# Odd mixer of an encoder kernel: both halves of a pair's scores as one bound run

## The chip, the cores and the metric

The kernel runs on one core of a Trainium2 chip. The metric is the device time of one execution in microseconds, as the median of several runs. A profiled execution gives a trace besides: its span goes from the first to the last instruction of the program.

The engines are named as the profile names them: PE is TensorE (matrix products; PEld is its loading of weights), DVE is VectorE, ACT is ScalarE, POOL is GpSimd, SP is the queue that issues most loads.

## What is computed

The program is a four-part encoder layer, twice: feed-forward, token mixer, attention into a memory, feed-forward, each followed by a layer norm. There are 512 tokens of width 1024, in 8 rows of 64 columns. The change lies in the token mixer of the second layer (the odd one), a neighbourhood attention with 16 heads of 64: each token looks at all 8 rows and at 16 columns around its own, with a learned bias.

```python
q, k, v = jnp.split(h @ w_in, 3, axis=-1)
...
s = jnp.einsum('bwhd,bawjhd->bhwaj', q_r, k_nb).astype(jnp.float32) * scale
s = s + bias.astype(jnp.float32)[None]
p = jax.nn.softmax(s.reshape(B, C_HEADS, GRID_W, kh * kw), axis=-1)
...
return jnp.einsum('bhwaj,bawjhd->bwhd', p, v_nb)
```

## The kernel before

**Precision.** Operands are split into a high and a low part (`split`: ScalarE makes the high part, VectorE the rest), and a product is the sum of three, high by high, high by low, low by high.

**The odd mixer (`mixer_c`).** Heads go in pairs, eight of them. The two heads of a pair lie on partitions 0 to 63 and 64 to 127 of their tiles of queries and keys, so a product of one head uses half of TensorE's rows (the profile writes 64*128), and products of the two heads can stand side by side. Per pair the loop records: the keys of the next pair (`keys`, into a "t" bank), the transposes of this pair's softmax weights (`turned`, four "t" banks), the queries of the pair after next (`queries`, a "d" bank), the scores of the next pair (`weights_of`), this pair's attention products (`attend`, a "d" bank; 64 output columns per head, which the profile writes 128*64), and two blocks of values for a later pair (`values`, "t" banks; pairs 0 to 5). From pair 6 on parts of the output projection (`down_steps`) stand in place of the work that runs out.

**Scores.** The 512 queries are four blocks of 128 tokens (16 columns of 8 rows). Block t meets `C_BLOCKS[t]`: 24 or 32 columns of keys, so products of 192 or 256 columns. Two blocks make a half, with one PSUM bank per head. Each block takes three products per head, and the two heads alternate: 12 products a half. VectorE adds the bias and finds the smallest value (`tensor_tensor_reduce`; in the order of instructions below these rows are called ISA), and ScalarE takes the exponential.

**PSUM.** The eight banks are shared out by tag: `BUFS` gives "a" three, "d" two, "t" three.

**What sets the order.** The code above only records operations (line 160 issues them all, so that the profile shows one line, and groups go by tile). `plan` is a list scheduler: each engine has a queue of operations that can start, with costs from `cost`; a buffer of a tag is granted in the order in which tiles were recorded, when all users of its last tile are done; an operation can start when its operands and the buffers of the tiles it uses are there. `emit` plans once, works out due times and plans again, then issues.

**Bound runs.** `join(n)` binds the last n operations: each depends on the one before, the first (the leader) takes over all operands' waits of the others, and the others get rank -1, that is, they go first as soon as they can start. Buffers are not part of this: an operation waits for a buffer only if it is itself a user of a tile in it. Before the change each half of the scores is bound by itself (12), and the leader uses one of the half's two banks. The attention products are bound too (8), with one bank.

Of the kernel before, what the change touches and what calls it, by code (L numbers as in the profile page):

```python
# [65 lines left out]
class Graph:  # L66
# [118 lines left out]
    def join(self, n):  # L185

        run = self.ops[-n:]
        for prev, op in zip(run, run[1:]):
            run[0].deps |= op.deps.difference(run)
            op.deps.add(prev)  # L190
            op.rank = -1
        run[0].ns += self.TURN
        run[-1].ns += self.TURN

# [139 lines left out]
class Kernel:  # L334
# [953 lines left out]
    def mixer_c(self, ln_i, last):  # L1288
        nc, a = self.nc, self.a
# [37 lines left out]
        def biases(pair):  # L1327

            table, inner = self.t2(F32), self.t2(F32)
            got = []  # L1330
            for s in range(2):
                tab = table[:, s * 256 : s * 256 + 256]
                nc.gpsimd.dma_start(out=tab, in_=self.bias[2 * pair + s])
                outer = self.t2(F32)
                dst = [outer[:, 0:192], inner[:, s * 256 : s * 256 + 256], outer[:, 192:384]]
                for i, off in enumerate((64, 0, 0)):
                    n = dst[i].shape[1]
                    nc.gpsimd.tensor_tensor(
                        out=dst[i].rearrange("p (u r) -> p u r", r=8),
                        in0=self.near[:, i, : n // 8].rearrange("p (u o) -> p u o", o=1).broadcast_to([P, n // 8, 8]),  # L1340
                        in1=tab[:, off : off + n].rearrange("p (u r) -> p u r", r=8),
                        op=ALU.subtract,
                    )
                got.append(dst)
            return got

        def weights_of(pair):

            tables, q, k = biases(pair), qs.pop(pair), ks.pop(pair)
            both = [[self.t2(F32), self.t2(F32)] for _ in range(2)]  # L1350
            sums = [self.small(4, "l4") for _ in range(2)]
            us = [[], []]
            for z in both:
                nc.gpsimd.memset(z[0][:, 0:64], 0.0)
                nc.gpsimd.memset(z[1][:, 448:512], 0.0)
            for half in range(2):
                ps = [self.ps("a") for _ in range(2)]
                for t in (2 * half, 2 * half + 1):
                    kc, w, _ = C_BLOCKS[t]
                    lo, n = (t % 2) * 256, w * ROWS  # L1360
                    for i, (x, y) in enumerate(((0, 0), (0, 1), (1, 0))):
                        for s in range(2):
                            own = slice(64 * s, 64 * s + 64)
                            nc.tensor.matmul(
                                ps[s][:, lo : lo + n], q[x][own, t * P : (t + 1) * P], k[y][own, kc * 8 : kc * 8 + n],
                                start=i == 0 and t % 2 == 0, stop=i == 2, skip_group_check=True,
                            )
                nc.join(12)
                for t in (2 * half, 2 * half + 1):
                    _, w, kind = C_BLOCKS[t]  # L1370
                    lo, n = (t % 2) * 256, w * ROWS
                    c0 = lo + (64 if t == 0 else 0)
                    for s in range(2):
                        u = both[s][half][:, c0 : c0 + n]
                        mn = self.small(1, "mn")
                        nc.vector.tensor_tensor_reduce(
                            out=u, in0=ps[s][:, lo : lo + n], in1=tables[s][kind], scale=1.0, scalar=3e38, op0=ALU.add,
                            op1=ALU.min, accum_out=mn,
                        )
                        nc.scalar.activation(u, u, AF.Exp, bias=mn, scale=-1.0, accum_out=sums[s][:, t : t + 1])  # L1380
                        us[s].append(u)
            for l, u4 in zip(sums, us):
                nc.vector.reciprocal(l, l)
                for t, u in enumerate(u4):
                    self.normalise(u, l[:, t : t + 1])
            return [[z[:, c * 256 : c * 256 + 256] for z in pair for c in range(2)] for pair in both]
# [50 lines left out]
        keys(0, True)  # L1437
        queries(1)
        us = weights_of(0)
        for pair in range(8):  # L1440


            if pair < 7:
                keys(pair + 1)
            else:
                steps(4)
            pts = turned(us)
            if pair < 6:
                queries(pair + 2)
            else:  # L1450
                steps(5 if pair == 6 else 3)
            if pair < 7:
                us = weights_of(pair + 1)
            if pair == 5:
                out.append(self.staged(self.down_steps(hs, w_out, 0, 256, 1.0 / ALPHA, [], False, alone=True)))
                steps(3)
            attend(pts, pair)
            if pair == 6:
                self.memory_tokens()
            if pair < 6:  # L1460
                for t in range(2):
                    values(pair // 2 + 1, 2 * (pair % 2) + t)
            elif pair == 6:
                steps(4)
# [242 lines left out]
```

## Time and profile before

| what | value |
|---|---|
| median of 3 runs | 2109.37 us (2108.8 to 2109.52) |
| profiled execution | 2108.22 us |
| its span | 2106.4 us |
| TensorE busy | 2086.6 us, 99% |
| VectorE busy | 1754.1 us, 83% |
| ScalarE busy | 1149.9 us, 55% |
| GpSimd busy | 308.4 us, 15% |
| granted TensorE clock | 0.998 |

TensorE is the engine that has almost no idle time. Products are pipelined: a record lasts longer than the distance to the next one, so the rate is read from starts, not from durations. In a timeline a row gives the start in microseconds from the span's start, the length from the first start to the last end of the records that it merges, engine, line, operation, tile written <- tiles read, and the count; a bracket gives the idle time ahead and what ended it.

### The profile page before, as it was taken

Reading aid. Unit: us, or ns where it says so; the run is one execution under the profiler, and the core shown is the slowest. Engines: PE = TensorE matmul, PEld = TensorE weight load, DVE = VectorE, ACT = ScalarE, POOL = GpSimd, SP = SyncE. Lnnn points to the kernel's source line nnn. Section 1 sums busy time; section 2 is a strip of 40 time slices with the busy share of each in tenths; the row PEclk is TensorE's granted clock in tenths of the full one; section 3 lists DMA queues with packets and bytes.
Section 4 is the critical chain, followed back from the end, with each engine's and each line's share of the span. In section 5 each row is a group of like instructions: output and inputs, shape, how many; then the busy total and the mean of one; then the engine's idle time right before and its main releaser. Section 6 shows DMA issues by size and latency. Waiting matters only on the chain.

```text
span 2106.4 us, 33063 instructions
## 1 busy us (share of the span) xinstructions
PE 2086.6 (99%) x13044; PEld 1847.4 (88%) x13044; DVE 1754.1 (83%) x2515; ACT 1149.9 (55%) x1847; POOL 308.4 (15%) x389
## 2 busy tenths in 40 slices
PE   9999999999999999999999999999999999999997
PEld 7999988777888999998999999888878889989996
DVE  7789988788758999998999999754487489999996
ACT  5555543697555655544554545346564466544551
POOL 0001015310002100000310000512131011100002
PEclk9999999999999999999999999999999999999999
DMA  7566562004443566555366656232234433566651
GB/s 208 154 156 153 138 192 84 21 21 140 130 126 95 140 158 183 116 146 165 105 150 161 149 123 189 80 106 76 99 85 148 141 100 115 126 155 156 148 143 60
DMA packets 207868, 270.70 MB, mean 129 GB/s; under 512 B 9184, under 2 KB 156256, under 8 KB 207712
## 3 DMA queue, kind: packets, MB, share of 16 engines
q1 hardware_dynamic: 171200, 211.69, 32.1%
q0 software_dynamic: 36224, 56.63, 15.4%
q8 instruction: 102, 1.67, 0.3%
q14 instruction: 54, 0.44, 0.1%
q10 hardware_dynamic: 288, 0.26, 0.0%
HBM read 266.46 MB, written 4.19 MB: 128 GB/s over the span
## 4 chain that ended last, share of the span: by engine, by line
PE 95%; DVE 3%; DMA 1%; issue 0%; ACT 0%; POOL 0%; DVEq 0%; ACTq 0%; POOLq 0%; SPq 0%
PE a L160 56%; PE d L160 23%; PE t L160 15%; DVE slab L160 1%; DMA slab<-ffn_w_up 1%; DVE x L160 1%; DMA slab<-ffn_w_gate 0%; ACT slab L160 0%; DVE t L160 0%; DVE xl L160 0%; DMA raw<-x_t 0%; POOL rms8y L160 0%; ACT junk L160 0%; POOL slab L160 0%; ACT t L160 0%
## 5 line engine op out<-in xcount | busy, mean ns | idle before, releaser
L160 DVE TENSOR_TENSOR slab<-slab,slab 128x1024 fp32r<-128x1024 f32 (+2 forms) x617 | 732.7, 1212 | 34.7 <-ACT slab L160 26.3
L160 PE MATMUL a<-slab,slab 128*128 128x256 f32 (+3 forms) x2480 | 592.9, 316 | 0.1
L160 ACT CAST slab<-slab 128x1024 fp32r<-128x1024 f32 (+2 forms) x457 | 465.9, 1038 | 180.2 <-DVE slab L160 75.9
L160 PE MATMUL a<-xh,slab 128*128 128x256 f32 (+2 forms) x2384 | 518.1, 307 | 0.3 <-ACT slab L160 0.3
L160 PE MATMUL a<-raw,slab 128*128 128x256 f32 x2432 | 460.9, 283 | 4.6 <-DVE t L160 4.1
L160 PEld LDWEIGHTS a<-slab,slab 128*128 128x128 f32 (+1 forms) x2480 | 422.2, 190 | 41.8 <-issue 3.6
L160 PEld LDWEIGHTS a<-xh,slab 128*128 128x128 f32 x2384 | 395.3, 191 | 26.2 <-ACT slab L160 1.2
L160 PEld LDWEIGHTS a<-raw,slab 128*128 128x128 f32 x2432 | 388.6, 192 | 11.8 <-DVE t L160 6.0
L160 PE MATMUL a<-xl,slab 128*128 128x256 f32 (+2 forms) x1192 | 366.0, 307 | 0.0
L160 PE MATMUL d<-slab,t 128*128 128x512 f32 x1104 | 278.6, 392 | 0.0
L160 PEld LDWEIGHTS a<-xl,slab 128*128 128x128 f32 x1192 | 227.2, 191 | 14.2 <-DVE xl L160 0.2
L160 PEld LDWEIGHTS d<-slab,t 128*128 128x128 f32 x1104 | 199.9, 189 | 36.9 <-issue 0.4
L160 PE MATMUL t<-slab,t 128*128 128x512 f32 x828 | 208.9, 392 | 0.3 <-DVE x L160 0.3
L160 PEld LDWEIGHTS t<-slab,t 128*128 128x128 f32 x828 | 149.5, 189 | 27.7 <-issue 0.7
L160 DVE TENSOR_TENSOR slab<-raw,slab 128x1024 fp32r<-128x1024 f32 (+2 forms) x144 | 158.7, 1126 | 15.7 <-ACT slab L160 15.6
L160 PE MATMUL d<-slab,slab 128*128 128x512 f32 (+3 forms) x736 | 167.4, 416 | 0.0
L160 PEld LDWEIGHTS d<-slab,slab 128*128 128x128 f32 (+1 forms) x736 | 106.2, 170 | 35.4 <-issue 12.9
L160 ACT CAST slab<-raw 128x1024 fp32r<-128x1024 f32 (+1 forms) x128 | 120.2, 968 | 30.9 <-DMA raw<-ab_w_in 9.6
L160 DVE SCALAR_TENSOR_TENSOR x<-d,x 128x512 f32<-128x512 f32 x174 | 118.7, 685 | 19.9 <-PE d L160 18.6
L160 ACT COPY t<-a 128x512 f32<-128x512 f32 (+1 forms) x124 | 68.8, 559 | 115.2 <-PE a L160 73.2
L160 DVE TENSOR_TENSOR t<-a,t 128x512 f32<-128x512 f32 (+1 forms) x100 | 64.3, 645 | 54.8 <-PE a L160 47.3
L160 POOL DMA_DIRECT2D slab<-ffn_w_down x40 | 47.7, 1193 | 294.0 <-DVE slab L160 256.4
(131 smaller groups left out, 2410.1 us busy)
## 6 DMA issues: line engine op xcount, KB each, us to landing
slab<-ffn_w_gate SPq DMA_DIRECT2D x89, 512.0 KB
slab<-ffn_w_up SPq DMA_DIRECT2D x89, 512.0 KB
slab<-ffn_w_down SPq DMA_DIRECT2D x80, 512.0 KB
slab<-ffn_w_down POOLq DMA_DIRECT2D x40, 512.0 KB, 5.8
raw<-mem_w_kv SPq DMA_DIRECT2D x16, 1024.0 KB
slab<-ffn_w_gate POOLq DMA_DIRECT2D x19, 512.0 KB, 6.8
slab<-ffn_w_up POOLq DMA_DIRECT2D x19, 512.0 KB, 6.0
raw<-mem_w_q SPq DMA_DIRECT2D x8, 1024.0 KB
```

The costliest lines, as they stand in the source:

```text
L160: op.call = lambda: fn(*args, **kw)
```

## The change

Two edits. In `weights_of` a pair's scores take four banks at once, two of tag "a" for the first half and two of tag "t" for the second, and all 24 products are bound as one run (`join(24)`) ahead of the code that evacuates them. In `join` the leader is entered as a user of every tile that a member of the run uses; so the planner starts a bound run only when the buffers of all its products are granted. This second edit applies to the attention products too.

```diff
@@ join
+        for info in self.tiles.values():
+            if info["users"].intersection(run):
+                info["users"].add(run[0])
         run[0].ns += self.TURN
         run[-1].ns += self.TURN
@@ weights_of
-            for half in range(2):
-                ps = [self.ps("a") for _ in range(2)]
+            banks = [[self.ps(tag) for _ in range(2)] for tag in "at"]
+            for half, ps in enumerate(banks):
                 for t in (2 * half, 2 * half + 1):
                     kc, w, _ = C_BLOCKS[t]
...
-                nc.join(12)
+            nc.join(24)
+            for half, ps in enumerate(banks):
                 for t in (2 * half, 2 * half + 1):
                     _, w, kind = C_BLOCKS[t]
```

In the order of instructions a row is line, operation, tile written <- tiles read, and the shape of what is written. A tile's name is its tag and a number.

TensorE, scores of pair 1 before: a_2718 and a_2719 are the first half's banks of the two heads, a_2724 and a_2725 the second half's, d_2730 the attention products of pair 0.

```order
L160 MATMUL a_2718<-slab_2694,slab_2670 128x256
L160 MATMUL a_2719<-slab_2694,slab_2670 128x256
L160 MATMUL a_2724<-slab_2694,slab_2670 128x256
L160 MATMUL d_2730<-slab_2695,slab_2650 64x256
L160 MATMUL d_2730<-slab_2698,slab_2650 64x256
L160 MATMUL d_2730<-slab_2695,slab_2650 64x256
L160 MATMUL a_2725<-slab_2694,slab_2670 128x256
L160 MATMUL a_2724<-slab_2694,slab_2670 128x256
```

TensorE, the same place now, the run's middle and its end; t_2720 and t_2721 are the second half's banks.

```order
L160 MATMUL a_2718<-slab_2694,slab_2670 128x256
L160 MATMUL a_2719<-slab_2694,slab_2670 128x256
L160 MATMUL t_2720<-slab_2694,slab_2670 128x256
L160 MATMUL t_2721<-slab_2694,slab_2670 128x256
...
L160 MATMUL t_2720<-slab_2694,slab_2670 128x192
L160 MATMUL t_2721<-slab_2694,slab_2670 128x192
L160 MATMUL d_2730<-slab_2695,slab_2650 64x256
L160 MATMUL d_2730<-slab_2698,slab_2650 64x256
```

The second half stands directly behind the first, and the eight attention products stand together behind both. The same is so in pairs 2 to 6; in pair 0 four products of the next keys stood between the halves and are behind them now.

TensorE, pair 7 before: d_2981 is the output projection, d_3010 the attention products of pair 6.

```order
L160 MATMUL a_2999<-slab_2963,slab_2928 128x256
L160 MATMUL a_3004<-slab_2963,slab_2928 128x256
L160 MATMUL d_2981<-slab_2983,t_2904_2985 128x512
L160 MATMUL d_3010<-slab_2964,slab_2911 64x256
L160 MATMUL d_3010<-slab_2967,slab_2911 64x256
L160 MATMUL a_3005<-slab_2963,slab_2928 128x256
```

TensorE, pair 7 now, the run's end and what follows:

```order
L160 MATMUL t_3000<-slab_2963,slab_2928 128x192
L160 MATMUL t_3001<-slab_2963,slab_2928 128x192
L160 MATMUL d_3010<-slab_2964,slab_2911 64x256
...
L160 MATMUL d_3010<-slab_2964,slab_2911 64x2x128
L160 MATMUL d_3010<-slab_2967,slab_2911 64x2x128
L160 MATMUL d_2981<-slab_2983,t_2904_2985 128x512
L160 MATMUL d_2981<-slab_2984,t_2904_2985 128x512
```

The single product of the output projection went behind the attention products, to the five others of its bank.

VectorE, scores of pair 1 before; d_2706 holds queries, whose low part is split off.

```order
L160 ISA t_2633_2714,mn_2723<-a_2719,t_2628_2709 128x256
L160 ISA mn_2723 128x1
L160 ISA t_2633_2714,mn_2721<-a_2719,t_2630_2711 128x192
L160 ISA mn_2721 128x1
L160 SCALAR_TENSOR_TENSOR slab_2707<-d_2706,slab_2707 128x512
L160 ISA t_2632_2713,mn_2726<-a_2724,t_2628_2709 128x256
```

VectorE now:

```order
L160 ISA t_2631_2712,mn_2722<-a_2718,t_2629_2710 128x192
L160 ISA mn_2722 128x1
L160 ISA t_2632_2713,mn_2726<-t_2720,t_2628_2709 128x256
...
L160 ISA t_2633_2714,mn_2723<-a_2719,t_2630_2711 128x192
L160 ISA mn_2723 128x1
L160 RECIPROCAL l_2635_2716<-l_2635_2716 128x4
L160 SCALAR_TENSOR_TENSOR slab_2707<-d_2706,slab_2707 128x512
```

All eight readings of the scores now stand together, those of the "t" banks third to sixth, and the queries' split comes behind the eighth.

## The prediction

> **What bounds the kernel now.** I read the page's busy shares first, then the table of stretches over the odd mixer, then TensorE's timeline at the places that the change touches.
>
> ```profile
> PE 2086.6 (99%) x13044; PEld 1847.4 (88%) x13044; DVE 1754.1 (83%) x2515; ACT 1149.9 (55%) x1847; POOL 308.4 (15%) x389
> ```
>
> TensorE is busy for 2086.6 of 2106.4 us. So a microsecond of TensorE time is a microsecond of the kernel, unless it is handed to a wait further on. The next rows cut the odd mixer at the starts of the score runs of pairs 1, 2, 6 and 7; the last stretch ends with pair 7's attention products. Columns: stretch, length, then busy time of each engine.
>
> ```profile
> 1418.68:1441.51 22.83, 22.83 (x137) 18.33 (x137) 8.66 (x26) 12.21 (x33) 4.74 (x12) 1.00 0.19 58
> 1509.97:1532.80 22.83, 22.83 (x137) 18.33 (x136) 10.60 (x30) 12.82 (x35) 0.00 (x0) 1.00 0.14 47
> 1532.80:1557.02 24.22, 24.22 (x143) 19.43 (x142) 18.94 (x40) 19.59 (x45) 9.12 (x16) 1.00 0.44 98
> 1557.02:1577.49 20.47, 20.47 (x127) 15.37 (x127) 19.84 (x41) 14.12 (x34) 8.54 (x7) 1.00 0.18 53
> ```
>
> TensorE is never idle here (22.83 of 22.83) at a granted clock of 1.00, and the periods repeat. VectorE has two thirds of a period free in the early pairs (8.66 of 22.83), but almost nothing in the last one (19.84 of 20.47). The cost to look for is therefore inside TensorE's stream: products that are not at their best rate. Here is that stream at pair 1 (start, length from first start to last end, operation, count):
>
> ```profile
> 1418.36 0.39 PE L160 MATMUL d<-xh,slab 128*128 128x512 f32 x1
> 1418.68 1.07 PE L160 MATMUL a<-slab,slab 64*128 64x192 f32 x13
> 1419.68 1.08 PE L160 MATMUL d<-slab,slab 128*64 128x256 f32 x6
> 1420.68 0.93 PE L160 MATMUL a<-slab,slab 64*128 64x256 f32 x11
> 1421.55 1.51 PE L160 MATMUL d<-slab,slab 128*64 128x256 f32 x10
> 1422.98 0.50 PE L160 MATMUL t<-slab,xh 128*128 128x512 f32 x1
> ```
>
> The 24 score products (64*128: two heads, each on half of the array's rows) stand as 13 and 11, and the previous pair's attention products (128*64; 16 records for eight products) as 6 and 10 between them. Both counts are odd in twos: the 13th score product is the leader of the second half, without its partner on the other rows, and three attention products are one and a half twos. The whole group lasts 1422.98 - 1418.68 = 4.30 us.
>
> **The change part by part.** *The score run.* What does one step, a product of each head side by side, cost? A window that ends at 1419.2 cuts the first run after eight products:
>
> ```profile
> 1418.68 0.72 PE L160 MATMUL a<-slab,slab 64*128 64x192 f32 x8
> ```
>
> Eight end after 0.72 us and thirteen (three steps more) after 1.07: 0.117 us a step. From the first start of the run to the start of what follows it takes 1.00 us for 13 (seven steps) and 0.87 for 11 (six). Unbroken, 24 products are twelve steps: 1.00 + 5 x 0.117 = 1.59 us as the upper end. Three of these five steps are 192 columns wide instead of 256; if they shrink in proportion, 0.09 us goes: 1.50 as the lower end. I take 1.55, against 1.87 now.
>
> *The attention products.* An unbroken set of the same eight stands at the end of the mixer, after pair 7:
>
> ```profile
> 1575.61 1.95 PE L160 MATMUL d<-slab,slab 128*64 128x256 f32 x16
> 1577.49 0.50 PE L160 MATMUL a<-slab,slab 128*128 128x512 f32 x1
> ```
>
> It takes 1.88 us to the next start; split it takes 1.00 + 1.43 = 2.43. So in a full pair the group becomes 1.55 + 1.88 = 3.43 instead of 4.30 us: 0.87 saved, in each of pairs 1 to 6, whose stretches repeat: 5.22 us.
>
> *Pair 0 and pair 7* have other neighbours:
>
> ```profile
> 1403.14 0.39 PE L160 MATMUL d<-xl,slab 128*128 128x512 f32 x1
> 1403.37 0.39 PE L160 MATMUL d<-xh,slab 128*128 128x512 f32 x1
> 1403.68 1.07 PE L160 MATMUL a<-slab,slab 64*128 64x192 f32 x13
> 1404.68 0.50 PE L160 MATMUL t<-xh,slab 128*128 128x512 f32 x1
> 1405.02 0.40 PE L160 MATMUL t<-xl,slab 128*128 128x512 f32 x1
> ...
> 1405.81 0.93 PE L160 MATMUL a<-slab,slab 64*128 64x256 f32 x11
> 1406.67 0.50 PE L160 MATMUL t<-xl,slab 128*128 128x512 f32 x1
> 1407.01 0.62 PE L160 MATMUL t<-xh,slab 128*128 128x512 f32 x2
> ```
>
> In pair 0, four full products of the next keys stand between the halves, and one more ends the group: 1407.01 - 1403.68 = 3.33 us. Full products follow each other at 0.23 (1403.14 to 1403.37), the first after a score run at 0.34 (1404.68 to 1405.02). Unbroken: 1.55 + 0.34 + 4 x 0.23 = 2.81; 0.52 saved.
>
> ```profile
> 1557.02 1.07 PE L160 MATMUL a<-slab,slab 64*128 64x192 f32 x13
> 1558.02 0.50 PE L160 MATMUL d<-slab,t 128*128 128x512 f32 x1
> 1558.46 0.65 PE L160 MATMUL d<-slab,slab 128*64 128x256 f32 x4
> 1559.04 0.93 PE L160 MATMUL a<-slab,slab 64*128 64x256 f32 x11
> 1559.90 1.52 PE L160 MATMUL d<-slab,slab 128*64 128x256 f32 x12
> 1561.34 0.97 PE L160 MATMUL d<-slab,t 128*128 128x512 f32 x3
> ```
>
> In pair 7 a single full product and two attention products are between the halves: 4.32 us to 1561.34. The order now puts the single one behind the attention products at 0.23: 1.55 + 1.88 + 0.23 = 3.66; 0.66 saved. Sum: 5.22 + 0.52 + 0.66 = **6.4 us**.
>
> The Trainium skill (TensorEngine Tiling (Array Packing), Key Properties) says that a change of tiling mode drains TensorE. The rows agree that a change costs about 0.1 us a side (0.34 against 0.23 behind the run). By that rule alone, two changes fewer in pairs 0 to 6 and three in pair 7 would give 17 x 0.1 = 1.7 us; by the rows the products that run without a partner cost more than the drains.
>
> *The wait that is added.* The planner gives the leader its place only when two "a" and two "t" banks are free. Behind it in TensorE's order stand 23 products, the attention products and the values, and VectorE's softmax waits for them. What held the "t" banks before are transposes; their last copy, and the score run of pair 2 that follows, are
>
> ```profile
> 1436.81 0.59 ACT L160 COPY slab<-t 128x512 f32<-128x512 f32 x1 [0.99 <-PE t L160]
> 1441.51 1.07 PE L160 MATMUL a<-slab,slab 64*128 64x192 f32 x13
> ```
>
> The copy ends at 1437.40, 4.1 us ahead of the run. I cost the wait at nothing; without that cover it costs its length in each pair.
>
> *Who gets the "t" banks next.* VectorE's reading of the scores, and the projection after the two value blocks:
>
> ```profile
> 1419.67 0.42 DVE L160 CUSTOM_DVE_ANT_0 t<-a,t 128x256 f32<-128x256 f32 x1 [4.39 <-PE a L160]
> 1420.92 0.69 DVE L160 SCALAR_TENSOR_TENSOR slab<-d,slab 128x512 fp32r<-128x512 f32 x1
> 1428.69 0.40 PE L160 MATMUL t<-xh,slab 128*128 128x512 f32 x1
> ```
>
> Four readings take 1420.92 - 1419.67 = 1.25 us and begin 0.99 us after the run's start. All eight now stand together, those of the "t" banks third to sixth: done 0.99 + 6 x 0.31 = 2.9 us after the start. The first value block takes the third "t" bank; the second needs a score bank at 3.43 + (1428.69 - 1422.98) / 2 = 6.3 us. Slack 3.4 us: nothing. The queries' split (0.69) that stood between the readings is now behind them, done at 0.99 + 2.50 + 0.69 = 4.2 instead of 2.9 us; the scores that use it are a period away.
>
> *Moved pieces elsewhere.* One full product and one VectorE split change places at the end of the layer before, and two memsets and a bias load now stand ahead of a normalisation step on GpSimd. There
>
> ```profile
> 1367.01 0.70 DVE x L160 x2
> ...
> 1371.61 0.97 PE a L160 x4
> ```
>
> TensorE waits for this VectorE chain until 1371.61. The split leaves the chain, but the accumulation ahead of it waits for the same last products; I bound it at 0.3 us either way and take nothing.
>
> **The rivals.** *The gain stops at a later wait.* In the last feed-forward layer TensorE once waits for a load:
>
> ```profile
> 1873.05 8.04 DMA slab<-ffn_w_up
> ...
> 1884.68 0.38 PE L160 MATMUL a<-raw,slab 128*128 128x256 f32 x1 [1.64 <-DVE t L160]
> ```
>
> If that load kept its time while TensorE came 6.4 us earlier, the wait would be 8.0 us and the kernel would stay at 2109.4. Against it: the chain goes from TensorE to this load at 1873.05, so the load moves with TensorE.
>
> *VectorE becomes the bound at pair 7.* It is busy for 19.84 of 20.47 us there, and a stretch 0.66 us shorter leaves it none. That may keep pair 7's 0.66 us, and as much again if the layer's end waits behind it: 2109.4 - 6.4 + 1.3 = 2104.3. For it: 1532.80 on is dense as well (18.94 of 24.22). Against: TensorE has no idle time there yet.
>
> *Slower: the "t" banks hold up the value blocks.* The second value block stalls TensorE when the readings of the "t" banks end more than 6.3 us after the run's start, 3.4 us later than worked out. It costs more than the change saves beyond 6.4 / 6 = 1.07 us of stall in each of pairs 1 to 6. Weight splits of about 1.2 us each ahead of the readings would be needed, four or more of them; with a stall of 2 us it gives 2109.4 - 6.4 + 12 = 2115. The readings' fixed place right behind the run speaks against it. The Trainium skill's PSUM Bottleneck (same page, Performance Considerations) names this risk: tiling speeds TensorE up, not the evacuation of PSUM.
>
> *The change doesn't do what it says*, so that runs stay broken (0, since 2109.4): TensorE's order shows all eight runs whole, so I leave it out of the chances.
>
> **How the numbers follow.** The profiled execution took 2108.22 us (span 2106.4), 1.15 below the median of 2109.37. The saving is the same in either: 2101.8 for the profiled one, 2109.4 - 6.4 = **2103.0 us** for the median. Own range of this case: 0.05 x 8 = 0.4 us for the run's length, 0.3 for the layer's start, and up to 0.7 lost at pair 7: 2102.3 to 2104.4. Chances: this case 0.76; VectorE the bound at pair 7, 0.09; gain stopped later, wholly or for the most part, 0.10; slower by the "t" banks 0.05. Two in ten may lie outside, so the range reaches some way into the cases of lost gain, and below for small gains that I didn't count: 2101.3 to 2106.5. A measurement here tells about 0.2% (4.2 us) from no change: faster is all of the first two but a little, 0.83; the same 0.12; slower 0.05.
>
> **What would show it.** Right: score runs of 24 records of about 1.6 us with 16 attention records behind them, period 22.83 down to about 21.96, TensorE still without idle time from 1376 on, its busy time lower by about 6 us. Wrong: releasers "DVE mn" or "DVE t" on TensorE's first products of the second value block; a wait at 1873 to 1885 that grew; or unbroken runs that take 1.8 us or more, which would mean that a product without its partner costs less than the rows say.

## The result, and the profile after

| | before | after |
|---|---|---|
| median, measured side by side | 2109.09 us (2106.62 to 2110.19) | 2101.70 us (2100.09 to 2102.65) |
| span of the profiled execution | 2106.4 us | 2099.5 us |
| TensorE busy | 2086.6 us | 2079.6 us |

The ratio is 0.9966 (95% interval 0.9956 to 0.9977): 7.2 us less, between 4.9 and 9.3. Forecast were 2103.0 us, 6.4 less than before. In the experiments below one of the ten runs of the odd split took 3439.74 us at a granted clock of 0.555; its ratio leaves that run out. The page's first part and the table of stretches, cut as before at the starts of the score runs (pair 0; pair 1; pairs 1 to 5 together; pair 6; pair 7 with its attention products):

```profile
PE 2079.6 (99%) x13044; PEld 1845.4 (88%) x13044; DVE 1754.5 (84%) x2515; ACT 1149.1 (55%) x1847; POOL 307.7 (15%) x389
```

```profile
1404.76:1419.33 14.57, 14.57 (x91) 11.89 (x90) 5.36 (x22) 10.45 (x29) 4.89 (x12) 1.00 0.21 67
1419.33:1441.25 21.92, 21.92 (x139) 17.99 (x138) 8.66 (x26) 12.27 (x33) 4.74 (x12) 1.00 0.19 61
1419.33:1528.94 109.61, 109.61 (x682) 89.93 (x681) 49.82 (x142) 65.94 (x175) 19.00 (x48) 1.00 0.26 87
1528.94:1552.27 23.33, 23.33 (x145) 19.07 (x144) 19.71 (x40) 19.54 (x44) 8.79 (x16) 1.00 0.47 116
1552.27:1572.06 19.79, 19.79 (x128) 15.29 (x127) 19.63 (x41) 13.94 (x34) 8.23 (x6) 1.00 0.13 39
```

The same two stretches of the kernel before that the prediction did not show, pair 0 and pairs 1 to 5 together:

```profile
1403.68:1418.68 15.00, 15.00 (x90) 12.10 (x90) 5.49 (x22) 10.56 (x29) 4.83 (x12) 1.00 0.20 64
1418.68:1532.80 114.12, 114.12 (x681) 91.63 (x680) 50.02 (x142) 65.93 (x175) 18.96 (x48) 1.00 0.26 84
```

TensorE is still busy without a gap in every stretch, at a clock of 1.00, with the same number of products in the program (13044); they stand closer. Saved are 15.00 - 14.57 = 0.43 us in pair 0, 114.12 - 109.61 = 4.51 in pairs 1 to 5, 24.22 - 23.33 = 0.89 in pair 6 and 20.47 - 19.79 = 0.68 in pair 7: 6.51 us in the mixer. TensorE's timeline at pair 1 shows the run whole:

```profile
1419.33 0.96 PE L160 MATMUL a<-slab,slab 64*128 64x192 f32 x12
1420.12 0.84 PE L160 MATMUL t<-slab,slab 64*128 64x256 f32 x12
1420.89 1.95 PE L160 MATMUL d<-slab,slab 128*64 128x256 f32 x16
1422.76 0.50 PE L160 MATMUL t<-slab,xh 128*128 128x512 f32 x1
```

24 score products take 1420.89 - 1419.33 = 1.56 us to the next start, the attention products behind them 1422.76 - 1420.89 = 1.87, the group 3.43.

### The profile page after: what moved, and what is told of

Its sections match the earlier page's. It is cut to its first block, busy times and chain, and to the rows that moved or that the text cites. A ratio compares the mean times of both kernels' runs of the same rounds, so it can differ in the third digit from the quotient of the medians.

```text
span 2099.5 us, 33054 instructions
## 1 busy us (share of the span) xinstructions
PE 2079.6 (99%) x13044; PEld 1845.4 (88%) x13044; DVE 1754.5 (84%) x2515; ACT 1149.1 (55%) x1847; POOL 307.7 (15%) x389
## 4 chain that ended last, share of the span: by engine, by line
PE 94%; DVE 3%; issue 1%; DMA 1%; ACT 1%; POOL 0%; DVEq 0%; ACTq 0%; POOLq 0%
PE a L160 55%; PE d L160 23%; PE t L160 16%; DVE slab L160 1%; DMA slab<-ffn_w_up 1%; DVE x L160 1%; ACT slab L160 0%; DVE t L160 0%; DVE xl L160 0%; DMA raw<-x_t 0%; POOL rms8y L160 0%; ACT junk L160 0%; POOL slab L160 0%; ACT t L160 0%; POOL lny L160 0%
## 5 line engine op out<-in xcount | busy, mean ns | idle before, releaser
L160 PE MATMUL a<-slab,slab 128*128 128x256 f32 (+3 forms) x2384 | 584.6, 317 | 0.1
L160 PEld LDWEIGHTS a<-slab,slab 128*128 128x128 f32 (+1 forms) x2384 | 415.3, 190 | 38.8 <-issue 3.6
```

What stands on the lines that cost most here:

```text
L160: op.call = lambda: fn(*args, **kw)
```

## Experiments

Because the mixer starts at different times from trace to trace, even where the order of instructions up to it is the same (below), the experiments are compared in two measures: the median against the kernel before on the same chip, and the length of pairs 1 to 5 in the trace, from one run's start to another's.

| kernel | median, us | kernel before beside it | ratio (95%) | pairs 1 to 5, us |
|---|---|---|---|---|
| before | | | 1 | 114.12 |
| changed | 2101.70 | 2109.09 | 0.9966 (0.9956 to 0.9977) | 109.61 |
| even split | 2104.09 | 2108.04 | 0.9983 (0.9973 to 0.9992) | 111.35 |
| odd split | 2108.31 | 2108.04 | 1.0000 (0.9990 to 1.0009) | 114.13 |
| leader edit alone | 2104.18 | 2108.04 | 0.9980 (0.9970 to 0.9989) | 110.63 |
| banks edit alone | 2100.59 | 2108.49 | 0.9965 (0.9952 to 0.9977) | 109.64 |
| scores head by head | 2110.89 | 2108.04 | 1.0012 (1.0002 to 1.0021) | 114.79 |
| attention head by head | 2108.80 | 2108.11 | 1.0005 (0.9996 to 1.0015) | 114.22 |
| attention first | 2102.07 | 2108.11 | 0.9967 (0.9955 to 0.9980) | 109.68 |
| late readings, planner blind | 2114.08 | 2108.11 | 1.0028 (1.0018 to 1.0037) | 121.50 |
| late readings, planner told | 2101.63 | 2108.11 | 0.9968 (0.9956 to 0.9980) | 109.94 |

**What was it that the broken runs lost?** My theory was that products without a partner on the other half of the array carry most of it; the rival, that the changes of shape between score and attention products do. Two kernels part them. Both bind scores and attention products into one run on the four banks; they differ only in how many of each stand together. `join` takes the bound operations as a second argument here; s are the 24 score products, p the 8 attention products. The lines are those of the even split; the odd one has 13 and 3 in place of 12 and 4.

```diff
             nc.join(24)
+            self.scored = nc.ops[-24:]
...
-            nc.join(8)
+            if pair < 7:
+                s, p = self.scored, nc.ops[-8:]
+                nc.join(32, s[:12] + p[:4] + s[12:] + p[4:])
+            else:
+                nc.join(8)
```

> In pairs 1 to 7 the group is bound as 12 score products, 4 attention products, 12 and 4: as many changes between score and attention products as in the kernel before, but no product without a partner. My theory (the lone products carry most of the loss): against the changed kernel only two more changes a pair, about 0.27 us by the rows (0.18 of the scores' 0.31 and 0.09 of the attention products' 0.56); period of pair 1 about 22.2 us instead of 21.92, and 7 x 0.27 = 1.9 us in all, so about 5 us faster than the kernel before. Rival (the changes alone carry it, 0.43 us each): period 22.8 us and no more than 1 us faster than the kernel before.

> Bound as 13, 3, 11 and 5 on the same four banks: the order of the kernel before in pairs 1 to 7, with pair 0 whole. My theory: all of those pairs' gain is lost again, 7 x 0.87 = 6.1 us, period of pair 1 about 22.8 us, so within 1 us of the kernel before; the four banks by themselves are worth nothing. Rival (the changes alone, at the 0.13 us a change that the rows show): as the even split, period 22.2 us and about 5 us faster than the kernel before.

TensorE's timeline at pair 1, the even split and then the odd one, each with the stretch of pairs 1 to 5:

```profile
1417.84 0.96 PE L160 MATMUL a<-slab,slab 64*128 64x192 f32 x12
1418.73 1.08 PE L160 MATMUL d<-slab,slab 128*64 128x256 f32 x8
1419.74 0.93 PE L160 MATMUL t<-slab,slab 64*128 64x256 f32 x12
1420.60 1.08 PE L160 MATMUL d<-slab,slab 128*64 128x256 f32 x8
1421.62 0.50 PE L160 MATMUL t<-slab,xh 128*128 128x512 f32 x1
...
1417.84:1529.19 111.35, 111.35 (x682) 89.76 (x682) 50.26 (x142) 66.11 (x175) 19.06 (x48) 1.00 0.26 86
```

```profile
1420.13 0.28 PE L160 MATMUL t<-slab,slab 64*128 64x256 f32 x1
1420.34 1.08 PE L160 MATMUL d<-slab,slab 128*64 128x256 f32 x6
1421.35 0.93 PE L160 MATMUL t<-slab,slab 64*128 64x256 f32 x11
1422.21 1.51 PE L160 MATMUL d<-slab,slab 128*64 128x256 f32 x10
1423.65 0.50 PE L160 MATMUL t<-slab,xh 128*128 128x512 f32 x1
...
1419.34:1533.47 114.13, 114.13 (x682) 91.64 (x682) 50.51 (x142) 66.67 (x175) 18.98 (x48) 1.00 0.25 84
```

The odd split has the length of the kernel before, to 0.01 us in five pairs, and its median within the noise: the four banks by themselves are worth nothing, the order is all. The even split, with the same number of changes, is 114.13 - 111.35 = 2.78 us shorter. So of the 4.51 us that the change saves in these pairs, 2.78 (0.56 a pair) come from lone products and 111.35 - 109.61 = 1.74 (0.35 a pair, 0.17 for each of two changes) from changes. That is more for the changes than the 0.27 a pair expected, and the median gained 4.0 us where about 5 were expected. The lengths in the rows show the lone products directly: six attention records last 1.08 us in the odd split, as long as eight in the even one, and 11 score products 0.93 us, as long as 12. A step of scores is 0.117 us; a step of attention records is (1.51 - 1.08) / 2 = 0.22, since ten records take six steps and six take four. One of the first and two of the second make 0.55 of the 0.56. Neither cause alone would do; the rival that changes carry it all (0.43 each) falls.

**Each edit alone.** First the leader's edit on the old code (two halves, three "a" banks, `join(12)`):

```diff
+        for info in self.tiles.values():
+            if info["users"].intersection(run):
+                info["users"].add(run[0])
```

> The two halves stay on the three banks of the kernel before and bound apart; only the edit of the leader is made. The leader of the second half now waits until its buffers are free, so that the order becomes 12 score products, 8 attention products, 12 score products. My theory: no lone product is left and one change more than in the changed kernel, 0.1 to 0.2 us a pair: period of pair 1 about 22.05 us; in pair 0 two changes, 0.25 us; pairs 6 and 7 are ordered anew, within 1 us either way. About 5.5 us faster than the kernel before (4 to 6.5). Rival (the gain needs the four banks, since scores that come in two runs keep VectorE and the softmax late): less than half of it, under 3 us faster.

TensorE at pair 1, the stretch of pairs 1 to 5, and that of pair 7 with the one product in it that waits:

```profile
1422.01 0.95 PE L160 MATMUL a<-slab,slab 64*128 64x192 f32 x12
1422.89 1.95 PE L160 MATMUL d<-slab,slab 128*64 128x256 f32 x16
1424.77 0.94 PE L160 MATMUL a<-slab,slab 64*128 64x256 f32 x12
...
1422.01:1532.64 110.63, 110.63 (x682) 90.23 (x682) 51.17 (x142) 65.24 (x175) 19.83 (x48) 1.00 0.26 86
...
1556.13:1577.24 21.11, 20.43 (x128) 15.31 (x127) 20.28 (x41) 14.12 (x34) 6.97 (x5) 1.00 0.19 71
...
1572.19 1.19 PE L160 MATMUL d<-slab,t 128*128 128x512 f32 x4 [0.68 <-DVE t L160]
```

The order is the expected 12, 8, 12. Pairs 1 to 5 save 114.12 - 110.63 = 3.49 us; the one change more than in the changed kernel costs (110.63 - 109.61) / 5 = 0.20. The rival that the gain needs four banks falls. Still the median gained only 3.9 us, just below the 4 to 6.5 expected: pair 7 became 21.11 - 20.47 = 0.64 us longer, since its new order lets TensorE wait 0.68 us for VectorE (busy 20.28 of 21.11 us). With pair 0 (14.87 us, 0.13 saved) and pair 6 (23.49, 0.73 saved) the mixer saves 0.13 + 3.49 + 0.73 - 0.64 = 3.71 us in this trace. The traced run itself took 2108.21 us, the longest of ten: its mixer starts late, at 1407.14 instead of 1403.68.

Then the other edit: four banks and one run of 24, without the three lines above.

> Only the first edit of the change: four banks and one bound run of 24, without the edit that makes the leader wait for the buffers of all its products. The order of instructions on every engine comes out the same as with it, since at the leader's turn all four banks stand free. My theory: the time of the changed kernel, 6.4 to 7.5 us faster than the kernel before; period of pair 1 21.92 us, runs of 24. Rival (the leader's wait does part of the work): a period between 21.92 and 22.83 us and broken runs.

```profile
1419.26 0.96 PE L160 MATMUL a<-slab,slab 64*128 64x192 f32 x12
1420.05 0.84 PE L160 MATMUL t<-slab,slab 64*128 64x256 f32 x12
1420.82 1.95 PE L160 MATMUL d<-slab,slab 128*64 128x256 f32 x16
...
1419.26:1528.90 109.64, 109.64 (x681) 89.93 (x680) 49.85 (x142) 65.97 (x175) 19.04 (x48) 1.00 0.26 87
```

It is the changed kernel: in the two traces every engine has the same instructions in the same order. So in this program the edits are not two halves of one gain: with four banks the leader's wait changes no instruction's place, and alone, on the old banks, it gave 3.49 of the 4.51 us in pairs 1 to 5.

**What a partner is worth.** If a lone product costs a whole step, 24 products in the order of the heads should cost 24 steps.

```diff
-            for half, ps in enumerate(banks):
-                for t in (2 * half, 2 * half + 1):
+            for s in range(2):
+                own = slice(64 * s, 64 * s + 64)
+                for t in range(4):
...
                     for i, (x, y) in enumerate(((0, 0), (0, 1), (1, 0))):
-                        for s in range(2):
...
```

> The changed kernel with the 24 score products of a run in another order: all of one head, then all of the other, so that no product has its partner on the other rows; changes as in the changed kernel. My theory: 12 steps more of 0.11 us a run, 1.3 us; the run takes 2.85 us instead of 1.56, period of pair 1 about 23.2 us, 8 x 1.3 = 10.5 us in all: about 3.5 us slower than the kernel before. Rival (what costs is the change of shape, not the missing partner): run 1.56 us, 7 us faster than the kernel before.

```profile
1422.60 0.95 PE L160 MATMUL a<-slab,slab 64*128 64x192 f32 x6
1423.40 0.52 PE L160 MATMUL t<-slab,slab 64*128 64x256 f32 x3
1423.64 0.35 PE L160 MATMUL a<-slab,slab 64*128 64x192 f32 x1
1423.76 0.25 PE L160 MATMUL t<-slab,slab 64*128 64x192 f32 x1
1423.84 0.27 PE L160 MATMUL a<-slab,slab 64*128 64x192 f32 x1
1423.85 0.28 PE L160 MATMUL t<-slab,slab 64*128 64x192 f32 x1
1423.95 0.27 PE L160 MATMUL a<-slab,slab 64*128 64x192 f32 x1
1423.96 0.27 PE L160 MATMUL t<-slab,slab 64*128 64x192 f32 x1
1424.06 0.54 PE L160 MATMUL a<-slab,slab 64*128 64x256 f32 x3
1424.44 0.83 PE L160 MATMUL t<-slab,slab 64*128 64x256 f32 x6
1425.20 1.95 PE L160 MATMUL d<-slab,slab 128*64 128x256 f32 x16
```

The run takes 1425.20 - 1422.60 = 2.60 us, 1.04 more than in turn, not 1.3: eight steps of 0.116 and 0.11, not twelve steps. The rows say why. Nine products of the first head (six "a", three "t") stand ahead of 1423.64; there, beside the ninth, the second head's first product ("a" again) starts, although three products of the first head precede it in the program, and these three ("t", 1423.76, 1423.85, 1423.96) run beside the second head's. TensorE reached three products ahead for the half of the array that stood free, so that four products have a partner. Most of the 0.11 lies at the second head's start, where its second product follows the first after 0.20 us (1423.64, 1423.84). The same test on the attention products followed:

```diff
-            for j in range(4):
-                for s in range(2):
+            for s in range(2):
+                for j in range(4):
```

> The changed kernel with the attention products of a run in another order: the four of one head, then the four of the other (8 records each). In the run of scores in head order, the second head's products began up to three products ahead, on the rows that stood free, so that 9 and not 12 steps were added, at 0.116 us. My theory: the same holds here at 0.21 us a record; if three records overlap, 5 steps are added, 1.05 us a pair; if three whole products (six records), 2 steps, 0.42 us. Period of pair 1 between 22.3 and 23.0 us, 8 pairs: 3.4 to 8.4 us slower than the changed kernel. Rival (no overlap across heads unless they alternate): 8 steps, 1.7 us, period 23.6, 13 us slower. Rival (a partner is worth nothing): 21.92.

The second row is the same run in a window that ends at 1420.73:

```profile
1419.81 2.86 PE L160 MATMUL d<-slab,slab 128*64 128x256 f32 x16
1419.81 1.35 PE L160 MATMUL d<-slab,slab 128*64 128x256 f32 x6
1422.60 0.50 PE L160 MATMUL t<-slab,xh 128*128 128x512 f32 x1
...
1418.24:1532.46 114.22, 114.22 (x681) 93.38 (x680) 49.91 (x142) 66.08 (x175) 19.00 (x48) 1.00 0.25 84
```

2.79 us instead of 1.87: 0.92 more, which is four steps of 0.22 and 0.05, far from the eight steps of no overlap. One behind the other, five records would have begun by 1420.73, 0.92 us after the first; six have. The sixth to start is the second head's first: it runs beside the first head's fifth, three records ahead of its turn, so that four records have a partner and four steps are added (the expectation's five left out the record beside which the second head starts). For the attention products, two records each, the reach is therefore three records and not three whole products. The Trainium skill (TensorEngine Tiling (Array Packing), Key Properties) says that different tiles can execute in parallel, independently; both traces agree, and show a reach of three records (a score product is one). In the kernel before, six attention records lay between the 13th score product and its partner, and it ran alone (the partner starts at 1420.68 in the prediction's rows); six is beyond that reach, so it stays open whether TensorE would reach across a change of shape.

**Does the direction of a change matter?** The attention products bound ahead of the scores (the line of the even split, and what stands in its place):

```diff
-                nc.join(32, s[:12] + p[:4] + s[12:] + p[4:])
+                nc.join(32, p + s)
```

> The eight attention products ahead of the 24 score products, bound together; three changes a pair as in the changed kernel, no lone product. My theory: a change costs about the same in either direction (0.17 us each in the even split), so the period of pair 1 stays at 21.9 us within 0.1 and the time within 1 us of the changed kernel. Rival (one direction is dearer): the period moves by 0.1 to 0.2 us, up to 1.5 us in all, either way.

Pairs 1 to 5 take 109.68 us (1419.45 to 1529.13) against 109.61, the median is 2102.07. Each of a group's three changes is turned round here, and their sum stays the same; what a single one costs in each direction this does not tell apart.

**The rival on the slower side.** To see how far the "t" banks are from holding up the second value block, their readings were put off: the "a" banks are read five times over, and the readings of the second half depend on these. The line `if again:` and the one below it stand only in the kernel whose planner is blind to the cost.

```diff
+                        for again in range(5 if half == 0 and 1 <= pair <= 5 else 1):
+                            nc.vector.tensor_tensor_reduce(
...
+                            if again:
+                                nc.ops[-1].ns = 0.0
+                            if half == 0:
+                                first.append(nc.ops[-1])
+                            else:
+                                nc.ops[-1].deps.update(first)
```

> The changed kernel; in pairs 1 to 5 VectorE reads the two 'a' banks five times over (16 readings more, 0.32 us each, results unchanged) before it reads the 't' banks, and the planner is told that this costs nothing, so that TensorE's order stays. It puts the readings of the 't' banks off by about 5.6 us: from 3.0 to 8.6 us after the run's start, past the second value block's start at 6.1 us. By the rival of the prediction (the 't' banks hold up the second value block) TensorE then stalls there for 1.9 to 2.5 us in each of five pairs, 10 to 12 us in all: about 4 us slower than the kernel before, and the slack of the changed kernel is as worked out. If the block had another bank to go to: no stall, as the changed kernel.

> The same 16 readings, but the planner knows their cost and puts ten products of the next queries ahead of the second value block (2.3 us of cover). My theory: the stall of the run before is gone but for a few tenths, within 1.5 us of the changed kernel. Rival (the order helps nothing, the banks are late for whatever stands there): the same 10 to 12 us.

First the changed kernel's VectorE: the first reading, the last one of a "t" bank, and the queries' split behind all eight. Then the blind kernel: VectorE's second reading of the "t" bank that is free first, and the product of the second value block that waits for it.

```profile
1420.32 0.42 DVE L160 CUSTOM_DVE_ANT_0 t<-a,t 128x256 f32<-128x256 f32 x1 [4.40 <-PE a L160]
...
1421.96 0.35 DVE L160 CUSTOM_DVE_ANT_0 t<-t,t 128x192 f32<-128x192 f32 x1
...
1422.95 0.66 DVE L160 SCALAR_TENSOR_TENSOR slab<-d,slab 128x512 fp32r<-128x512 f32 x1
```

```profile
1426.20 0.36 DVE L160 CUSTOM_DVE_ANT_0 t<-t,t 128x192 f32<-128x192 f32 x1
...
1426.62 0.50 PE L160 MATMUL t<-slab,xh 128*128 128x512 f32 x1 [1.45 <-DVE mn L160]
...
1418.63:1540.13 121.50, 112.50 (x683) 89.67 (x682) 74.87 (x302) 65.38 (x175) 22.02 (x48) 1.00 0.24 79
```

The mechanism is there: the block waits 1.45 us, and so in all five pairs (7.6 us of waits by VectorE's "mn" together). The single wait is less than the 1.9 us worked out, because one bank is free after two readings and not after four. Pairs 1 to 5 grow by 121.50 - 109.61 = 11.9 us. That this lies within the 10 to 12 expected is luck in part: TensorE is idle for 121.50 - 112.50 = 9.0 us, the 7.6 of these waits and 1.4 at transposes behind them, which the expectation did not count, and its busy time grows by 112.50 - 109.61 = 2.9 us, part of it where products start anew behind a wait (the first of the block takes 0.33 us to the next start); the rest is not traced. The Trainium skill's PSUM Bottleneck (same page, Performance Considerations) names this risk, and 5 us of readings more make it real here: they turn a kernel that gains 7 into one that loses 6. In the changed kernel the readings of the "t" banks end at 1421.96 + 0.35 = 1422.31, 2.98 us after the run's start.

Told of the cost, the planner puts ten products of the next queries ahead of the block:

```profile
1426.38 0.62 PE L160 MATMUL d<-xh,slab 128*128 128x512 f32 x2
1426.83 0.39 PE L160 MATMUL t<-slab,xh 128*128 128x512 f32 x1
...
1418.20:1528.14 109.94, 109.94 (x681) 90.04 (x680) 74.55 (x302) 67.47 (x175) 23.59 (x48) 1.00 0.26 87
```

No wait is left, the five pairs are 109.94 - 109.61 = 0.33 us longer, and the median is the changed kernel's. The rival would therefore need readings that are late and that the planner doesn't expect.

## Why the prediction was right

The sign, the mechanism and the range (2101.3 to 2106.5) held. The median of 2101.7 us is 1.3 below the forecast and 0.6 below the main case's own range (2102.3 to 2104.4); the trace's own sum for the mixer is 0.1 us off. Of the 1.3 us the kernel before makes 0.3 (2109.09 beside the change, 2109.37 in the forecast) and the mixer 0.1; the other 0.9 is less than the interval of the gain (4.9 to 9.3) leaves open, and what it is the runs do not show.

- **The score run**: 1.55 us predicted, 1.56 measured. The forecast took the middle between 1.50 and 1.59, so an agreement to 0.01 us is luck in part. **The attention products**: 1.88 predicted, 1.87 measured. The group: 3.43 and 3.43.
- **The sum**: 5.22 in pairs 1 to 6 against 4.51 + 0.89 = 5.40; a period saves 0.90 us and not 0.87. The 0.03 more lies outside the group, between 1422.76 and the next run; what it is stays open. Pair 0: 0.52 against 0.43; the group there takes 2.85 us, 0.04 more than predicted; the other 0.05 went behind it, where the transposes stand between other products than before (not tested). Pair 7: 0.66 against 0.68. In all 6.40 against 6.51.
- **The reason** (lone products cost more than the changes): right, 0.56 against 0.35 us a pair. The size of a change was too small: the forecast took about 0.1 us from a full product behind a score run and put it on all 17 changes, while the even split and the leader's edit showed 0.17 to 0.20 between score and attention products. The sum didn't notice, since it was made from whole pieces, before and unbroken. At that price, an estimate for the changes beside full products, the 17 would have given 17 x 0.17 = 2.9 us by themselves, not 1.7 and not the 6.5 of the trace.
- **The wait that is added** was costed at nothing, with 4.1 us of cover. The result is right and simpler than that: with the four banks the leader's wait changes no order here.
- **Who gets the "t" banks**: 2.9 us predicted for the readings, 2.98 measured; the queries' split done at 4.2, measured 1422.95 + 0.66 - 1419.33 = 4.28. The slack of 3.4 us was counted from the last reading of both banks; the block takes the first bank that is free. In the blind kernel that one is free 1426.20 + 0.36 - 1418.63 = 7.93 us after the run's start, in the changed kernel after two readings less, 1421.96 + 0.35 - 0.62 - 1419.33 = 2.36; of these 5.6 us 1.45 were waited, so the slack was about 4.1 us.
- **Gain that stops at a later wait**: no. The wait for the load did not grow:

```profile
1877.76 0.38 PE L160 MATMUL a<-raw,slab 128*128 128x256 f32 x1 [0.52 <-DVE t L160]
```

  It fell from 1.64 to 0.52 us. That can't be counted as a gain of the change: in the kernel with the attention products head by head, whose median is that of the kernel before, the same wait was 0.17 us. The spans differ by 6.9 us: the mixer starts 1404.76 - 1403.68 = 1.08 us later, is 6.51 shorter, and what follows it is 1.47 shorter, 1.12 of them at this wait.

- **VectorE the bound at pair 7**: not in the changed kernel, where TensorE is busy for 19.79 of 19.79 us; but VectorE, busy for 19.63, is close to it. The leader edit alone shows what happens when the order shifts: 0.68 us of waiting there. With the attention products first TensorE waits 0.52 us for VectorE right behind the mixer (at 1573.26).
- **Moved pieces before the mixer**, bounded at 0.3 us: not to be told from the traces. The first run starts at 1404.76 instead of 1403.68, but in the other kernels that have the changed kernel's order up to there it started anywhere from 1403.27 (even split) to 1407.00 (scores head by head).

## What to carry to other kernels

Where two products share the array, look for odd counts in the timeline: a run that breaks after its 13th product costs the step of the one left over on both sides of the break, which here was more than the two changes of shape. Price such a repair by whole pieces of the trace, an unbroken set of the same products where there is one and a step read from a longer run where there is none, not by a cost per break: the pieces gave the group to 0.01 us, the cost per break a quarter of the gain. And see in the instructions' order which of several edits moves anything, since beside the four banks the leader's wait moved nothing.

## What the runs showed that was not expected

- TensorE starts a product on the free half of the array up to three records ahead of its turn (scores head by head: 1.04 us more a run instead of 1.3; attention products: 0.92 instead of 1.7). Strict alternation of the heads is therefore worth less than a full doubling.
- A change between score and attention products costs 0.17 us as the mean of both directions (even split), and one more change 0.20 (leader's edit).
- Between traces the mixer's start scatters by 3.7 us (1403.27 to 1407.00) with the same order up to it, and the late wait behind a load between 0.17 and 1.64 us. A change of 0.3% is seen in one trace only stage by stage.
